# A hybrid decoder step on one core: another chunk order in round one, another place for the spatial products, top-ks given out together, other PSUM for the key transpositions, and weight splits off GpSimd

## The chip, the cores and the metric

The kernel runs on one core of a Trainium2 chip. The metric is the device time of one execution in microseconds (us). The engines are PE (matrix products; PEld is its weight load), DVE (vector), ACT (scalar functions), POOL (GpSimd) and SP (which here only issues DMAs). Each engine works through its own list of instructions in order, and waits on semaphores where it needs another's result.

## The reference

One layer of a decoder step for 2048 prompt rows and 64 sample rows (8 sequences of 8), model width 1024, in float32:

```
z = rmsnorm(x) @ w_in                     # q, k, v, index queries qi, index key ki, index weights wi, ga, u, vm, gm
score = sum_h wi_h * relu(qi_h . ki)      # 8 index heads of 64
idx = top_k(causal score, 256)            # per query row
o = softmax attention of 8 heads over the chosen keys (4 key heads, QK norm, partial rotary)
s = W_s (lower triangular 128 x 128, per group) @ layernorm(gelu(vm)) + b_s
gm_out = gelu(u) * s * silu(gm)
r = x + [o * silu(ga), gm_out] @ w_out
y = r + sigmoid(rmsnorm(r) @ w_ple_gate) * (p @ w_ple_proj)
```

The outputs are y for both sets of rows, the new k, v and index keys, and the layernormed vm of the sample rows.

## The kernel before, in words

**Phase A, projection.** The 16 prompt blocks of 128 rows and the sample block (SB) are done in three rounds (`ROUNDS`). In each round the columns of w_in are taken in 14 chunks (`CH`): x1, x2 (index key and queries), vm0, vm1, k, v, u0, u1, gm0, gm1, q0, q1, ga0, ga1. A chunk has 256 columns, x1 has 328 from two places of w_in. Every float32 product is made of halves rounded to the PE's fp32r and their remainders: `proj` issues 24 matmuls for one block and chunk (16 at L319 and L320, 8 at L322), and 16 for SB (L312, L313). In round one `load_w` fetches each chunk as 8 raw tiles (L282, five buffers), and splits each into the high half (L286 on ACT for every second tile of the first chunk, L288 on POOL otherwise) and the low half (L289 on DVE); later rounds reload the halves from DRAM. `split_h` transposes the rows of x (L250). `post` finishes a chunk: for v one ACT copy and a store (L409); for q0, q1 and k a square, a sum (L389), two small POOL steps (L390, L391), two products (L396, L397) and the rotary part (L133 to L136).

`spatial(g)` makes one group's spatial products (L338, L343) between the projections: four groups in the chunk v, four in u0.

**Index work.** From the end of x2 `pump` gives out, after each block and by a credit, index products of the due blocks (L688, L689 on PE, relu L691 on ACT, accumulation L693 on DVE) and top-ks (`topk`: seven counts, L829 on ACT with small DVE steps between them, then MAX8 at L865 and a mask, L875, whose store goes to `s_mask`).

**End of phase A.** The products of the gm columns with w_out follow (`gm_split` L567, `gm_product` L579 to L583, eviction L585, store L588). At the ninth, `pump(1e9)` gives out all that is left of the index work, and `prep_early` begins: per key block loads (L991, L992, two buffers each), a doubling copy on ACT (L1015), four transpositions on PE (L1021), evictions into Kst on ACT (L1023) and DVE (L1024), and two POOL steps for the values (L1026, L1027, tile Vst). The transposes take their PSUM from the pool `tp`, two buffers, which `gm_split` uses too. Kst and Vst lie where the index work's tiles lay. A flag (L897, L902) sums up the top-ks' counts.

**Phase B** is the attention over query blocks; **phase C** the product with w_out, the norm, and the gate, whose ten weight tiles `raw_split` (L1421 on ACT, L1423 and L1424 on POOL or DVE) splits between the blocks, and where POOL adds the residual (L1437).

The program's order is only the scheduler's input: the framework simulates the program's times and writes each engine's list from that.

Of the kernel before, what the change touches and what calls it, by code (L numbers as in the profile page):

```python
# [9 lines left out]
F32 = mybir.dt.float32  # L10
# [44 lines left out]
Q_POOL = [0, 0, 1]  # L55
ROUNDS = [[0, 1, 2, 3, 4, SB], [5, 6, 7, 8, 9, 10], [11, 12, 13, 14, 15]]
DUE = ROUNDS[:2] + [ROUNDS[2][::-1]]
CH = [
# [53 lines left out]
class Builder:  # L112
# [85 lines left out]
    def phase_a(self, eb):  # L198
        tc, nc, I, O = self.tc, self.nc, self.I, self.O
        with ExitStack() as es:  # L200
# [68 lines left out]
            def load_w(ci, r):  # L269
# [8 lines left out]
                for k in range(8):  # L278
# [5 lines left out]
                    g = self.gk[:, k:k + 1]  # L284
                    if ci == 0 and k % 2:
                        nc.scalar.activation(wh[:, k], raw, AF.Copy, scale=g)  # L286
                    else:
                        nc.gpsimd.tensor_scalar(wh[:, k], raw, g, 1.0, op0=OP.mult, op1=OP.mult)  # L288
# [163 lines left out]
            def pump(budget):  # L452
                credit[0] = min(credit[0], 0.0) + budget
                while credit[0] > 0 and (blocks_due or primed or dots or tops):
# [10 lines left out]
                    if l:  # L465
                        try:
                            v = next(l[0])
                            steps[0] += l is dots
                            if isinstance(v, tuple):
                                tops.append(self.topk(*v))  # L470
                                v = 0
                            credit[0] -= v
                            if l is tops and not (dots or primed or blocks_due):
# [3 lines left out]

            seq = [(r, c) for r in range(len(ROUNDS)) for c in range(len(CH))]
            load_x(ROUNDS[0][0])
            W0 = load_w(0, 0)  # L480
            split_h(ROUNDS[0][0])
# [10 lines left out]
            for si, (r, c) in enumerate(seq):  # L492
                blocks = ROUNDS[r]
                name = CH[c][0]
# [31 lines left out]
                for j, b in enumerate(blocks):  # L526
# [9 lines left out]
                    post(name, b, z)  # L536
                    g = {"v": j + 4 - len(blocks), "u0": 4 + j if j < 4 else -1}.get(name, -1)
                    if g >= 0:
# [11 lines left out]
                cur = nxt  # L550
                if c == 1:
                    blocks_due += [b for b in DUE[r] if b >= 2]
                    tot = sum((b + 1) * 18 + 8 if b < SB else 110 for b in blocks if 2 <= b)
                    self.idx_rate = tot / (RATE[r] * len(blocks))
# [37 lines left out]
            for n in range(0, 17, 2):  # L592
# [5 lines left out]
                for j in range(2):  # L598
                    for b in order[n:n + 2]:
# [9 lines left out]
                        if u == DRAIN:  # L609
                            pump(1e9)  # L610
                            ei.close()
                            early = self.prep_early(eb, lambda: self.tp.tile([128, 4, 128], F32, name="tp"))
                        if u == FLAG_AT:
# [777 lines left out]
    def phase_c(self):  # L1391
# [3 lines left out]
        with ExitStack() as es:  # L1395
# [145 lines left out]
            for n in range(LEAD + 1):  # L1541
# [3 lines left out]
                for q in range(n * per, min(n * per + per, len(gates))):  # L1545
                    raw_split(*gates[q], nc.gpsimd if q % 3 == 2 else nc.scalar, nc.gpsimd if q % 3 == 1 else V)
                    if q + 3 < len(gates):
                        raw_load(*gates[q + 3])
# [38 lines left out]
```

## Time and profile before

| | us |
|---|---|
| median of 3 runs | 1889.77 (1889.49 to 1900.7) |
| the profiled execution's own time | 1893.5 |
| its span | 1891.7 |
| PE busy in the span | 1833.5 (97%) |
| mean granted PE clock | 0.988 of 2.4 GHz |
| chain that ended last | PE 83%, DVE 5%, DMA 5%, POOL 2%, issue 2%, ACT 2% |

The profile shows one execution. PE's busy time is counted from modelled ends, so a busy PE can still run at the lower of its two clock levels; the column for the clock tells that. Times in the rows count from the first instruction of the span.

### The profile page before, as it was taken

What the parts mean: (1) busy time and instruction counts of PE and PEld (TensorE: products, weight loads), DVE (VectorE), ACT (ScalarE), POOL (GpSimd) and SP (SyncE); (2) the same over time, 40 slices, a digit from 0 to 9 for tenths busy, and PEclk for the clock granted to TensorE, in tenths of its full rate; (3) what the DMA queues carried; (4) which work ended last, traced back from release to release, by engine and by line L of the source; (5) the groups of instructions that cost most, each with busy time, mean ns of one, the idle gap of its engine ahead of it and who ended that gap; (6) DMA issues with size and microseconds to landing.
All of it is one profiled execution on the core that took longest, in us unless ns stands there. A gap on an engine that the chain in (4) does not pass through costs nothing.

```text
span 1891.7 us, 33962 instructions
## 1 busy us (share of the span) xinstructions
PE 1833.5 (97%) x11974; PEld 1601.0 (85%) x11974; DVE 1242.1 (66%) x3631; ACT 1018.2 (54%) x1909; POOL 623.5 (33%) x950
## 2 busy tenths in 40 slices
PE   7989998999999999999988899999999999999998
PEld 7989988999999999999877678778777777888887
DVE  5597665378878547788752789888999764233321
ACT  4244335256565636766654888868788653122121
POOL 5482562342012324013303442233221364222221
PEclk9989999999999999999999899999999999999999
DMA  8855756645344554554553442233220373223211
GB/s 253 247 163 179 223 189 203 215 131 161 119 162 146 194 174 145 163 170 134 176 188 128 134 112 76 64 108 94 61 78 12 100 258 122 74 95 104 94 37 45
DMA packets 243806, 261.53 MB, mean 138 GB/s; under 512 B 83176, under 2 KB 209840, under 8 KB 243248
## 3 DMA queue, kind: packets, MB, share of 16 engines
q1 hardware_dynamic: 237744, 240.45, 40.5%
q0 software_dynamic: 5888, 18.88, 3.4%
q8 instruction: 95, 1.56, 0.3%
q14 instruction: 79, 0.65, 0.1%
HBM read 171.90 MB, written 87.37 MB: 137 GB/s over the span
## 4 chain that ended last, share of the span: by engine, by line
PE 83%; DVE 5%; DMA 5%; POOL 2%; issue 2%; ACT 2%; SPq 0%; DVEq 0%; POOLq 0%; ACTq 0%
PE z L319 10%; PE z L320 10%; PE z L322 10%; PE b_o L1155 7%; PE b_tp L1138 6%; PE c_mm L1471 5%; PE c_mm L1470 5%; PE c_mm L1474 5%; PE b_s L1103 3%; PE dots L688 3%; PE dots L689 3%; PE b_s L1104 3%; PE z L579 1%; PE z L580 1%; PE z L583 1%
## 5 line engine op out<-in xcount | busy, mean ns | idle before, releaser
L319 PE MATMUL z<-whi,hhi 128*128 128x256 f32 (+1 forms) x1792 | 463.0, 292 | 10.5 <-ACT vt L414 5.0
L320 PE MATMUL z<-wlo,hhi 128*128 128x256 f32 (+1 forms) x1792 | 454.1, 287 | 0.2 <-DVE wlo L289 0.2
L319 PEld LDWEIGHTS z<-whi,hhi 128*128 128x128 f32 x1792 | 341.9, 191 | 21.2 <-issue 8.5
L320 PEld LDWEIGHTS z<-wlo,hhi 128*128 128x128 f32 x1792 | 341.8, 191 | 6.1 <-DVE wlo L289 1.5
L322 PE MATMUL z<-whi,hlo 128*128 128x256 f32 (+1 forms) x1792 | 262.6, 286 | 0.0
L322 PEld LDWEIGHTS z<-whi,hlo 128*128 128x128 f32 x1792 | 237.7, 190 | 2.0
L693 DVE SCALAR_TENSOR_TENSOR big<-dots,sgn,big 128x1024 f32<-128x1024 f32 (+7 forms) x176 | 179.2, 1018 | 52.3 <-ACT dots L691 50.6
L125 DVE TENSOR_TENSOR b_pt<-b_tp,b_pt 128x512 fp32r<-128x512 f32 (+1 forms) x288 | 183.4, 655 | 12.1 <-ACT b_pt L124 11.0
L691 ACT ACTIVATE dots<-dots 128x1024 f32<-128x1024 f32 (+7 forms) x176 | 140.3, 801 | 87.7 <-PE dots L689 82.9
L1155 PE MATMUL b_o<-b_pt,Vst 128*128 128x512 f32 x544 | 184.1, 424 | 1.2 <-DVE b_pt L125 0.8
L124 ACT ACTIVATE b_pt<-b_tp 128x512 fp32r<-128x512 f32 (+1 forms) x288 | 155.5, 578 | 48.2 <-PE b_tp L1138 45.4
L1138 PE MATMUL b_tp<-mats,b_sm 128*128 128x128 f32 x1088 | 172.0, 275 | 2.3 <-DVE b_pt L125 1.8
L1112 ACT ACTIVATE b_sm<-b_sm,b_st 128x128 f32<-128x128 f32 (+15 forms) x128 | 154.7, 1210 | 16.2 <-DVE b_st L1105 15.4
L829 ACT ACTIVATE bfw<-big,tk 128x384 bf16<-128x384 f32 (+14 forms) x105 | 136.4, 1300 | 45.7 <-DVE tk L849 27.9
L1138 PEld LDWEIGHTS b_tp<-mats,b_sm 128*128 128x128 f32 x1088 | 131.5, 141 | 34.1 <-ACT b_sm L1112 4.8
L1103 PE MATMUL b_s<-Kst,b_qh 128*128 128x512 f32 (+3 forms) x320 | 139.5, 439 | 4.1 <-DVE b_st L1105 2.2
L1105 DVE CUSTOM_DVE_ANT_0 b_sm<-b_s,b_mask,b_st 128x512 f32<-128x512 f32 (+3 forms) x192 | 123.9, 646 | 22.6 <-PE b_s L1104 17.8
L1104 PE MATMUL b_s<-Kst,b_ql 128*128 128x512 f32 (+3 forms) x320 | 117.6, 370 | 0.0
L688 PE MATMUL dots<-ki_stack,qih 128*128 128x512 f32 (+3 forms) x304 | 113.0, 373 | 3.1 <-DVE mk L833 3.1
L689 PE MATMUL dots<-ki_stack,qil 128*128 128x512 f32 (+3 forms) x304 | 110.2, 371 | 0.0
L1471 PE MATMUL c_mm<-c_l_w_ple_gate,c_mh 128*128 128x512 f32 x272 | 106.7, 392 | 3.2 <-DVE c_l_w_ple_gate L1424 2.1
L1470 PE MATMUL c_mm<-c_h_w_ple_gate,c_mh 128*128 128x512 f32 x272 | 109.0, 401 | 0.0
(351 smaller groups left out, 3747.0 us busy)
## 6 DMA issues: line engine op xcount, KB each, us to landing
whi<-s_wh SPq DMA_DIRECT2D x52, 512.0 KB
wlo<-s_wl SPq DMA_DIRECT2D x52, 512.0 KB
raw<-w_in SPq DMA_DIRECT2D x112, 128.0 KB
s_wh<-whi SPq DMA_DIRECT2D x13, 1024.0 KB
s_wl<-wlo SPq DMA_DIRECT2D x13, 1024.0 KB
b_qr<-s_q SPq DMA_DIRECT2D x32, 256.0 KB
s_r<-hlo SPq DMA_DIRECT2D x32, 256.0 KB
c_r<-s_r SPq DMA_DIRECT2D x16, 512.0 KB
```

What stands on the lines that cost most here:

```text
L125: nc.vector.tensor_tensor(lo, src, hi.bitcast(F32), OP.subtract)
L319: nc.tensor.matmul(z, lhsT=hh[:, k], rhs=wh[:, k, :n], start=(k == 0), stop=False)
L320: nc.tensor.matmul(z, lhsT=hh[:, k], rhs=wl[:, k, :n], start=False, stop=False)
L322: nc.tensor.matmul(z, lhsT=hl[:, k], rhs=wh[:, k, :n], start=False, stop=(k == 7))
L688: nc.tensor.matmul(ps[:, s0:s0 + sn], lhsT=qh[h // 4][:, h % 4], rhs=rhs, start=True, stop=False)
L693: nc.vector.scalar_tensor_tensor(a, r, self.sgn[:, b, h:h + 1], a, op0=OP.mult, op1=OP.add)
L1103: nc.tensor.matmul(ps, lhsT=qh[:, h], rhs=rhs, start=True, stop=False)
L1104: nc.tensor.matmul(ps, lhsT=ql[:, h], rhs=rhs, start=False, stop=True)
L1138: nc.tensor.transpose(ps[:, k, r], sm2[r][:, (k0 + k) * 128:(k0 + k) * 128 + 128], ident)
L1155: nc.tensor.matmul(o.rearrange("p a b -> p (a b)"), lhsT=Vst[:, kb, g].rearrange("p a d -> p (a d)"), rhs=pt[:, k].rearrange("p a b -> p ( ...
L1470: nc.tensor.matmul(z, lhsT=hi[:, k], rhs=wts[k][0][:, ns], start=(k == 0), stop=False)
L1471: nc.tensor.matmul(z, lhsT=hi[:, k], rhs=wts[k][1][:, ns], start=False, stop=(b == SB and k == nk - 1))
```

## The change

It has six edits. In round one the chunks come in the order `FIRST`: v, x1, x2, vm0, vm1, k, q0, u0, u1, gm0, gm1, q1, ga0, ga1; rounds two and three keep theirs. In round one four spatial groups are called in q0, not in v. The index work still begins behind x2, which is now the third chunk; the constants that were made in the second and third chunk (index constants; `gmlp_weights`, `page_rows` with L190 and L191) are now made in x1 and x2. A step of `pump` is not charged to the credit once no index products are left. The key transpositions take their PSUM from the index products' pool (`dots`, two buffers). All ten weight tiles of phase C are split by ACT (high half) and DVE (low half).

```diff
--- before.py
+++ after.py
@@ -54,6 +54,7 @@
 WLO_DVE = [6, 5, 0]
 Q_POOL = [0, 0, 1]
 ROUNDS = [[0, 1, 2, 3, 4, SB], [5, 6, 7, 8, 9, 10], [11, 12, 13, 14, 15]]
+FIRST = [5, 0, 1, 2, 3, 4, 10, 6, 7, 8, 9, 11, 12, 13]
 DUE = ROUNDS[:2] + [ROUNDS[2][::-1]]
 CH = [
     ("x1", [(1536, 72), (1024, 256)]),
@@ -282,7 +283,7 @@
                         nc.sync.dma_start(raw[:, o:o + cn], I["w_in"][0, k * 128:(k + 1) * 128, c0:c0 + cn])
                         o += cn
                     g = self.gk[:, k:k + 1]
-                    if ci == 0 and k % 2:
+                    if ci == FIRST[0] and k % 2:
                         nc.scalar.activation(wh[:, k], raw, AF.Copy, scale=g)
                     else:
                         nc.gpsimd.tensor_scalar(wh[:, k], raw, g, 1.0, op0=OP.mult, op1=OP.mult)
@@ -469,15 +470,16 @@
                             if isinstance(v, tuple):
                                 tops.append(self.topk(*v))
                                 v = 0
-                            credit[0] -= v
+                            if dots or primed or blocks_due:
+                                credit[0] -= v
                             if l is tops and not (dots or primed or blocks_due):
                                 tops.append(tops.pop(0))
                         except StopIteration:
                             l.pop(0)
 
-            seq = [(r, c) for r in range(len(ROUNDS)) for c in range(len(CH))]
+            seq = [(r, c) for r in range(len(ROUNDS)) for c in (range(len(CH)) if r else FIRST)]
             load_x(ROUNDS[0][0])
-            W0 = load_w(0, 0)
+            W0 = load_w(FIRST[0], 0)
             split_h(ROUNDS[0][0])
             load_x(ROUNDS[0][1])
             ropet = ac.tile([128, 17, 32], F32, name="ropet")
@@ -534,7 +536,7 @@
                         f()
                     later.clear()
                     post(name, b, z)
-                    g = {"v": j + 4 - len(blocks), "u0": 4 + j if j < 4 else -1}.get(name, -1)
+                    g = {"v" if r else "q0": j + 4 - len(blocks), "u0": 4 + j if j < 4 else -1}.get(name, -1)
                     if g >= 0:
                         spatial(blocks, g)
                     if name == "ga1":
@@ -548,7 +550,7 @@
                         keep_w(c, cur)
                     pump(self.idx_rate)
                 cur = nxt
-                if c == 1:
+                if name == "x2":
                     blocks_due += [b for b in DUE[r] if b >= 2]
                     tot = sum((b + 1) * 18 + 8 if b < SB else 110 for b in blocks if 2 <= b)
                     self.idx_rate = tot / (RATE[r] * len(blocks))
@@ -609,7 +611,8 @@
                         if u == DRAIN:
                             pump(1e9)
                             ei.close()
-                            early = self.prep_early(eb, lambda: self.tp.tile([128, 4, 128], F32, name="tp"))
+                            early = self.prep_early(eb, lambda: self.dp.tile([128, 1024], F32, name="dots")[:, :512]
+                                                    .rearrange("p (a b) -> p a b", a=4))
                         if u == FLAG_AT:
                             self.flag(self.tp.tile([128, 4, 128], F32, name="tp")[:, 0])
                 for b in order[n + 2:n + 4]:
@@ -1543,7 +1546,7 @@
                 stage1b(blocks[n])
                 stage1a(blocks[n + 1])
                 for q in range(n * per, min(n * per + per, len(gates))):
-                    raw_split(*gates[q], nc.gpsimd if q % 3 == 2 else nc.scalar, nc.gpsimd if q % 3 == 1 else V)
+                    raw_split(*gates[q], nc.scalar, V)
                     if q + 3 < len(gates):
                         raw_load(*gates[q + 3])
             for n in range(2):
```

Lines of the changed kernel are one to three higher than those of before: L1021 is L1024 there, L567 is L569, L992 is L995.

On SP, the start of the program: x is the rows of a block (`big` holds two of them), raw a piece of the chunk's weights. Before:

```order
L232 DMA x_253<-x_prompt 128x1024
L282 DMA raw_257<-w_in 128x72
L282 DMA raw_257<-w_in 128x256
...
L282 DMA raw_292<-w_in 128x72
L282 DMA raw_292<-w_in 128x256
L232 DMA x_318<-x_prompt 128x1024
L484 DMA ropet_320<-c_rope 128x544
L232 DMA big_322<-x_prompt 128x1024 x2
L232 DMA big_325<-x_prompt 128x1024
L232 DMA big_325<-x_sample 64x1024
```

and now:

```order
L233 DMA x_253<-x_prompt 128x1024
L283 DMA raw_257<-w_in 128x256
...
L283 DMA raw_273<-w_in 128x256
L233 DMA x_310<-x_prompt 128x1024
L486 DMA ropet_312<-c_rope 128x544
L233 DMA big_314<-x_prompt 128x1024
L283 DMA raw_277<-w_in 128x256
L283 DMA raw_281<-w_in 128x256
L283 DMA raw_285<-w_in 128x256
L233 DMA big_314<-x_prompt 128x1024
L233 DMA big_317<-x_prompt 128x1024
L233 DMA big_317<-x_sample 64x1024
```

The first chunk is 8 transfers where it was 16, and the second block's rows are asked for ahead of the last three of them.

On PE, the end of phase A: `tp` and `dots` with one source b_kd are key transpositions (L1021, now L1024), `tp` from hlo the transposes of gm (L567, now L569), each z the first matmul of one of the w_out products of 12. Before:

```order
L1021 MATMUL tp_13027<-mats_60,b_kd_12993 128x128 x4
L579 MATMUL z_12870<-whi_12555,hhi_12815 128x512
...
L579 MATMUL z_12939<-whi_12399,hhi_12923 128x512
...
L579 MATMUL z_13040<-whi_12555,hhi_12931 128x512
...
L1021 MATMUL tp_13059<-mats_60,b_kd_13025 128x128 x4
L567 MATMUL tp_13073<-mats_60,hlo_13023 128x128 x4
L567 MATMUL tp_13081<-mats_60,hlo_13055 128x128 x4
L579 MATMUL z_13088<-whi_12399,hhi_13072 128x512
...
L1021 MATMUL tp_13105<-mats_60,b_kd_13057 128x128 x4
L579 MATMUL z_13118<-whi_12399,hhi_13080 128x512
...
L1021 MATMUL tp_13135<-mats_60,b_kd_13103 128x128 x4
```

and now:

```order
L1024 MATMUL dots_13027<-mats_60,b_kd_12993 128x128 x4
L581 MATMUL z_12838<-whi_12399,hhi_12815 128x512
...
L569 MATMUL tp_13073<-mats_60,hlo_13023 128x128 x4
...
L581 MATMUL z_12978<-whi_12399,hhi_12931 128x512
...
L569 MATMUL tp_13213<-mats_60,hlo_13163 128x128 x4
...
L581 MATMUL z_13180<-whi_12555,hhi_13080 128x512
...
L900 MATMUL tp_13398<-f_sm_13410 1x1
L1024 MATMUL dots_13059<-mats_60,b_kd_13025 128x128 x4
L1024 MATMUL dots_13105<-mats_60,b_kd_13057 128x128 x4
L581 MATMUL z_13228<-whi_12399,hhi_13212 128x512
...
L581 MATMUL z_13258<-whi_12399,hhi_13220 128x512
...
L1024 MATMUL dots_13135<-mats_60,b_kd_13103 128x128 x4
```

Between the second and the third key transposition stood five products, and stand eleven with six gm transposes; the third now follows the flag's product (`tp_13398`), and from there the keys come in pairs.

On SP, the same stretch: b_kr are key loads, b_vr value loads, s_r the products' stores. Before:

```order
L876 DMA s_mask_174<-bfw_12225 128x1536
L992 DMA b_vr_13005<-v_prompt 128x256
L992 DMA b_vr_13037<-v_prompt 128x256
L991 DMA b_kr_13144<-k_prompt 128x256
L992 DMA b_vr_13069<-v_prompt 128x256
...
L992 DMA b_vr_13209<-v_prompt 128x256
L588 DMA s_r10_167<-hlo_13023 128x512
L991 DMA b_kr_13176<-k_prompt 128x256
L992 DMA b_vr_13255<-v_prompt 128x256
L992 DMA b_vr_13285<-v_prompt 128x256
```

and now:

```order
L879 DMA s_mask_174<-bfw_12107 128x1536
L590 DMA s_r11_168<-hlo_13055 128x512
L995 DMA b_vr_13005<-v_prompt 128x256
...
L995 DMA b_vr_13115<-v_prompt 128x256
...
L994 DMA b_kr_13144<-k_prompt 128x256
...
L994 DMA b_kr_13176<-k_prompt 128x256
...
L995 DMA b_vr_13285<-v_prompt 128x256
L994 DMA b_kr_13208<-k_prompt 128x256
L994 DMA b_kr_13254<-k_prompt 128x256
...
L995 DMA b_vr_13395<-v_prompt 128x256
L994 DMA b_kr_13284<-k_prompt 128x256
```

The key loads still stand among the value loads of later blocks, in pairs now.

## Rows read from the trace of the kernel before

**Rows 1.** The page, part 1: busy us, share of the span, instructions.

```profile
PE 1833.5 (97%) x11974; PEld 1601.0 (85%) x11974; DVE 1242.1 (66%) x3631; ACT 1018.2 (54%) x1909; POOL 623.5 (33%) x950
```

**Rows 2.** PE's waits: line and tile, for what; us in total, times, longest.

```profile
PE tp L1021 <- DVE Kst L1024: 7.3, 2, 6.2
...
PE z L319 <- ACT vt L414: 5.0, 2, 2.5
...
PE tp L567 <- DVE Kst L1024: 3.4, 3, 1.8
...
PE dots L688 <- DVE mk L833: 3.1, 1, 3.1
...
PE z L319 <- DVE vt L316: 2.7, 1, 2.7
...
PE c_mm L1471 <- DVE c_l_w_ple_gate L1424: 2.1, 1, 2.1
...
PE c_mm L1471 <- POOL c_l_w_ple_gate L1424: 1.2, 1, 1.2
```

**Rows 3.** Timeline, SP's DMA issues at the start: start us, duration us, work.

```profile
2.28 8.27 SPq L282 DMA_DIRECT2D raw<-w_in  x16
...
10.60 0.43 SPq L232 DMA_DIRECT2D x<-x_prompt  x1
```

**Rows 4.** Timeline, PE at the start: the first block's first matmul, the next block's transposes.

```profile
7.72 0.61 PE L319 MATMUL z<-whi,hhi 128*128 128x328 f32 x1
...
17.30 1.06 PE L250 MATMUL tp<-mats,x 128*128 128x128 f32 x4
```

**Rows 5.** Windows: length, busy PE, PEld, DVE, ACT, POOL, then clock, DMA share, GB/s.

```profile
40.50:62.00 21.50, 16.65 (x107) 15.47 (x108) 13.21 (x43) 2.62 (x8) 12.46 (x31) 0.78 0.81 246
...
140.00:160.00 20.00, 20.00 (x158) 18.97 (x157) 15.00 (x72) 7.95 (x21) 7.78 (x12) 1.00 0.69 213
...
160.00:200.00 40.00, 40.00 (x311) 36.99 (x310) 30.15 (x132) 19.53 (x44) 9.30 (x17) 1.00 0.53 169
...
262.00:285.00 23.00, 23.00 (x160) 18.89 (x158) 15.29 (x49) 7.68 (x20) 12.71 (x19) 1.00 0.53 164
...
980.50:1045.10 64.60, 51.16 (x248) 41.21 (x247) 22.23 (x49) 27.47 (x51) 18.02 (x32) 0.92 0.37 121
```

**Rows 6.** Timeline, DVE: the addition for the sample rows of the first chunk.

```profile
43.55 0.49 DVE L316 TENSOR_TENSOR vt<-z,vt 64x328 f32<-64x328 f32 x1
```

**Rows 7.** Windows of the instructions on tile qn in 262 to 285: DVE, ACT, POOL.

```profile
262.00:285.00 23.00, 8.11 (x31) 2.84 (x6) 0.00 (x0) 1.00 0.53 164
```

**Rows 8.** The same window, instructions on tile qst: DVE, POOL.

```profile
262.00:285.00 23.00, 4.46 (x11) 7.47 (x11) 1.00 0.53 164
```

**Rows 9.** Timeline, PE: two key transpositions and the product between them.

```profile
993.51 0.60 PE L1021 MATMUL tp<-mats,b_kd 128*128 128x128 f32 x4
...
993.87 0.48 PE L579 MATMUL z<-whi,hhi 128*128 128x512 f32 x1
...
996.69 0.60 PE L1021 MATMUL tp<-mats,b_kd 128*128 128x128 f32 x4
```

**Rows 10.** Timeline, DVE: the first key evictions.

```profile
986.03 1.30 DVE L1024 TENSOR_TENSOR Kst<-tp,Kst 64x512 fp32r<-64x512 f32 x2
```

**Rows 11.** Tile b_vr: ns least, median, most; first and last start.

```profile
L1026 POOL TENSOR_SCALAR Vst<-b_vr x16: 397/404/406, 988.2 to 1015.4; 128x256 fp32r<-128x256 f32 x16
```

**Rows 12.** Timeline, SP: the issue of one key load.

```profile
1000.42 0.42 SPq L991 DMA_DIRECT2D b_kr<-k_prompt  x1
```

**Rows 13.** Timeline, ACT: the copy that waited for this load.

```profile
1003.55 0.62 ACT L1015 COPY b_kd<-b_kr 128x512 f32<-128x512 f32 x1 [2.39 <-DMA b_kr<-k_prompt]
```

**Rows 14.** Timeline, DVE: two low halves of phase C's weights.

```profile
1541.60 1.22 DVE L1424 TENSOR_TENSOR c_l_w_ple_gate<-c_raw,c_h_w_ple_gate 128x1024 fp32r<-128x1024 f32 x1
...
1559.69 3.38 DVE L1424 TENSOR_TENSOR c_l_w_ple_gate<-c_raw,c_h_w_ple_gate 128x1024 fp32r<-128x1024 f32 x1 [0.94 <-POOL c_h_w_ple_gate L1423]
```

**Rows 15.** Timeline, POOL: the addition beside the second of them.

```profile
1559.62 2.36 POOL L1437 TENSOR_TENSOR c_x<-c_x,c_r 128x1024 f32<-128x1024 f32 x1
```


## The prediction

> **What bounds the kernel now.** I read the page first: PE is busy for 1833.5 of 1891.7 us [rows 1], so only its 58 us of idle time, and the time in which it is busy at the lower of its two clock levels (1.2 instead of 2.4 GHz), can be won; an engine that is relieved elsewhere wins nothing. Then PE's list of waits, which says where the idle time lies [rows 2]. It is spread: the largest entries are key transpositions and gm transposes that wait for the key evictions (7.3 + 3.4 us, up to 6.2 at once), projections behind the s_ga stores (5.0), an index product in round one (3.1), a projection behind the sample rows of x1 (2.7), and phase C's gate products (2.1 + 1.2). Then the windows of the places that the change touches, where the reader is to compare PE's busy time with the length and look at the clock [rows 5], and the timelines around each of them.
>
> The sum is made against the profiled execution, 1893.5 us (span 1891.7), which is 3.7 us above the median of the three runs; I take the difference over to the median. A measurement of this kernel can tell about 1% from no change, that is 18.9 us.
>
> **Start, v as the first chunk.** SP spends from 2.28 to 10.55 us on the sixteen raw transfers of x1, and asks for the second block's rows only at 10.60 [rows 3]. The first block's 24 matmuls therefore last from 7.72 to 17.30, 9.58 us [rows 4]. In v there are 8 transfers, the second block's rows go ahead of the last three, and a matmul has 256 columns where it had 328: 9.58 x 256/328 = 7.5, a gain of 2.1 from the columns alone. But x1 is not gone, only second, and its columns are paid later; what is won is waiting time, not columns. I take +2, with bounds 0 (the weights come no faster) and 4.
>
> **The sample rows of x1.** In 40.5 to 62, PE is busy for 16.65 of 21.50 us, at a mean clock of 0.78 [rows 5]: 4.85 us idle, and about 0.22 x 16.65 = 3.7 us lost to the clock, 8.5 in all. The step that ended last is the addition for SB at 43.55 on DVE [rows 6], which in DVE's list stood behind the page rows (L190, L191) and low halves of the next weights; PE was stopped for 2.7 us of that [rows 2]. In the changed order the first chunk ends in ACT copies, x1 is second, and the page rows are made a chunk later, in x2. The stop for SB should go, but the same small work is still to be done in the first 80 us, so something is late elsewhere. I take +3, bounds -1 and 7.
>
> **Spatial products from v to q0.** Their number is unchanged, and so is their place relative to k, the chunk ahead. The 3.1 us stop of the index products behind a count's DVE step [rows 2] belongs to that place too, and I cost it at nothing. What is new is that q0 stands where v stood. v costs DVE nothing there; q0 costs, per block, six of the 31 instructions on qn, 8.11/31 x 6 = 1.57 us, and one sum, of the 4.46 us on qst, about 0.41 [rows 7, 8]: 1.98, for six blocks 11.9 us. POOL gets 7.47/11 x 2 = 1.36 per block, 8.1 in all [rows 8]. In the 20 us of v's chunk DVE is busy for 15.0, in the 40 us behind it for 30.2 [rows 5]. 15.0 + 11.9 = 26.9 us do not fit in 20; 57.0 fit into the 60, barely. The 6.9 us that are too much must slip into the next chunk. PE is kept waiting as far as two z buffers don't cover it, and each stop also costs clock. I take -4; the bounds are -12 (6.9 and as much again of low clock) and +2 (all covered, and a gap at k's end closed by the shift). Where q0 was, PE had no idle time to give back (23.00 of 23.00 busy at clock 1.00 [rows 5]): nothing returns there.
>
> By the Trainium skill (SBUF — State Buffer, section "SBUF: two separate sides") a DVE instruction with two SBUF inputs and a GpSimd instruction that reads SBUF exclude each other for their whole length. By that, q0 could cost DVE up to POOL's 1.36 us more per block, 8 us in six, and this term would be -12. The rows of q0's old place speak against so much: there the same DVE work ran beside the same POOL work at 8.11/31 = 0.26 us an instruction, and PE never stopped [rows 5, 7, 8].
>
> **Unchanged places.** The stops behind the s_ga stores and the first small blocks of phase B have the same work and the same queues: nothing.
>
> **Credit.** The last top-ks are given out together. The last one is a chain of counts, each waiting for the one before, and its start is set by the last index product, which doesn't move. Nothing, bounds -2 and 2.
>
> **End of phase A.** This is the main term. In 980.5 to 1045.1, PE is busy for 51.2 of 64.6 us, at a clock of 0.92 [rows 5]. The work in it is 12 products of 2.82 us (993.87 to 996.69), 14 key transpositions and 7 gm transposes of 0.36 each (993.51 to 993.87) [rows 9], and two sample products that I put at 1.9: 33.8 + 7.6 + 3.8 = 45.2 us. So 19.4 us are lost. The cause is the PSUM: the first two key transpositions hold both `tp` buffers until the first key evictions on DVE at 986.03 [rows 10], which come only when the last top-k is through and its memory is free. Until then neither a third key nor a gm transpose can start, and the products run out.
>
> With the keys in `dots`, the gm transposes have `tp` for themselves. The order of the changed kernel puts eleven products and six transposes between the second and third key, 11 x 2.82 + 6 x 0.36 = 33 us from about 961, so that PE comes to the third key near 994, some 8 us after the first evictions. From there 14 key transpositions are left, 8 products and two for the samples: 14 x 0.36 + 8 x 2.82 + 3.8 + 0.4 = 32 us. Everything at full speed would end near 1026, 19 us earlier.
>
> What is late next would be the key loads, since they stand on SP among value loads, whose buffers come free only by POOL's steps for the values: sixteen starts from 988.2 to 1015.4, 1.8 us apart [rows 11]. A key takes 3.1 us from its issue to its copy (1000.42 to 1003.55) [rows 12, 13]. SP's new order shows the closest case: the loads of the ninth and tenth key (b_kr_13208 and the next) stand behind the eleventh value's (b_vr_13285), which with two buffers waits for the ninth value step, 988.2 + 9 x 1.8 = 1004.4; they can be used near 1008. PE gets to them near 994 + 6 x 0.36 + 5 x 2.82 = 1010. That holds, with little in hand. I take +14 of the 19.4: 5 us for waits that an order doesn't show. Bounds 6 (the keys hold up each pair by 2 us) and 19.
>
> **Phase C.** The two waits of the gate products are 2.1 and 1.2 us [rows 2]. POOL no longer splits, so it starts its additions earlier, and the raw buffers come free earlier. DVE has three more low halves of 1.22 us, ACT three more high halves; both have room there. I take +3, bounds 1 and 4. The wait of 2.1 us ended with a low half on DVE that took 3.38 where another took 1.22 [rows 14], while POOL added the residual for 2.36 beside it [rows 15]; the lower bound is for a low half that still meets an addition and is 2.2 late. The same page and section of the Trainium skill speaks against this edit, since POOL keeps its additions and all low halves now go to the engine that they exclude. The trace agrees here (3.38 against 1.22 + 2.36); by the rule of the Trainium skill alone this term would be +1.
>
> **Sum.** 2 + 3 - 4 + 0 + 14 + 3 = 18 us. The profiled execution would take 1893.5 - 18 = 1875.5, and the median 1889.8 - 18 = 1872 us, 0.95% less.
>
> **The rivals.**
> - *DVE becomes the bound in q0* (slower than before). If the products of q0 find no free z, PE runs its 20 us at half clock, 20 us lost. For it: DVE's load of 26.9 in 20 us, and the clock that falls at each stop, as in 40.5 to 62 [rows 5]. Against it: the scheduler may spread the work, and q0's old place ran with no idle time. With 2 for the early terms together, 13 at the end of A and 1 in phase C: 2 - 20 + 13 + 1 = -4, about 1894. It decides once DVE's work per block, index work included, exceeds what PE takes for one, 20/6 = 3.3 us. The rule of the Trainium skill quoted above (SBUF — State Buffer) points the same way. Chance 0.10.
> - *The stop moves to the key loads.* The value steps wait for the last mask's store, so the loads can begin no earlier than before; if each pair then waits 2 us, the end of A brings 6, and the sum is 10: 1880. Chance 0.16.
> - *All of it works.* 19 at the end of A, 3 + 5 early, 0 in q0, 3 in C: 30, or 1860. For it: the order puts 8 us between the evictions and the third key. Chance 0.20.
> - *The change doesn't do what it says.* The engines' orders come from simulated times; if these err as they did before, stops of the same size come at other places, and only C's 3 us remain: 1887. Chance 0.10.
> - The forecast, with its own range of 1865 to 1879: chance 0.44.
>
> **The numbers.** 1872 us. The range for 8 in 10 is 1858 to 1888: it leaves out the slow rival and a part of the best one. Faster by over 1% means below 1870.9: the whole of the third rival and half of the forecast's case, with a little of the rest, 0.44. Slower by over 1% needs more than 1908.7: the first rival with every other term at its low end, 0.03. The rest, 0.53, is within 1%.
>
> **What would show it.** In the profile after: the wait of the key transpositions for Kst is gone or below 2 us, and the stretch from the last top-k's MAX8 to phase B's first score is near 50 us, not 64.6. In q0's chunk of round one PE has idle time and a lower clock, with DVE over 9 tenths. The first block takes about 7.5 us. The gate products wait for under 1 us. The forecast is wrong if the gm products in turn wait for their own evictions or loads, or if the q0 stop exceeds 12 us.

## The result, and the profile after

The changed kernel takes 1877.5 us in the median of 8 runs (1875.3 to 1881.5), the kernel before in the same series 1892.2; the ratio is 0.9919 with a 95% interval from 0.9904 to 0.9935, so 0.8% less, 14.7 us, where 18 were forecast. The profiled execution takes 1878.1 us, its span 1876.1.

Part 1 of its page, against [rows 1]:

```profile
PE 1826.7 (97%) x11974; PEld 1595.9 (85%) x11974; DVE 1243.8 (66%) x3634; ACT 1018.5 (54%) x1912; POOL 607.3 (32%) x944
```

PE's work is the same 11974 matmuls; its span is 15.6 us shorter. PE's list of waits, against [rows 2] (line numbers are one to three higher):

```profile
PE z L320 <- DVE qn L380: 3.9, 2, 2.9
...
PE dots L691 <- DVE mk L836: 2.5, 1, 2.5
...
PE z L320 <- ACT vt L410: 2.3, 1, 2.3
...
PE c_mm L1473 <- ACT c_ph L125: 2.2, 1, 2.2
...
PE c_mm L1474 <- DVE c_l_w_ple_gate L1427: 1.2, 2, 0.8
```

From the last top-k's MAX8 (979.88) to phase B's first score (1025.94) it takes 46.1 us, where it took 64.5. No wait for Kst is left, where there were 7.3 + 3.4 us, and the s_ga wait (vt L414, 5.0 us) is gone from the head of the list; in their place stand small stops of round one (L380, L410) and a new one in phase C, for c_ph. The windows that answer to [rows 5], with 300 to 320 added:

```profile
40.50:62.00 21.50, 18.23 (x117) 17.33 (x117) 10.93 (x45) 5.22 (x22) 9.90 (x24) 1.00 0.85 283
...
160.00:200.00 40.00, 39.56 (x300) 36.53 (x299) 33.29 (x149) 20.76 (x50) 20.75 (x29) 1.00 0.55 174
...
300.00:320.00 20.00, 19.46 (x161) 18.64 (x160) 4.42 (x15) 8.60 (x21) 2.15 (x6) 1.00 0.60 208
...
980.50:1026.00 45.50, 44.99 (x231) 36.62 (x229) 17.56 (x43) 24.14 (x46) 18.16 (x32) 1.00 0.52 171
```

and that stretch in the kernel before, where two stops of 2.5 us lay:

```profile
300.00:320.00 20.00, 15.04 (x122) 14.63 (x121) 8.73 (x50) 11.78 (x24) 1.02 (x3) 0.97 0.78 265
```

To see where time came from and went, I set against each stretch what its matmuls would take at full speed (for each shape of matmul the spacing that three in ten of them undercut in the trace of before) and call the rest lost. This is an estimate. Its gains add up to 15.5 of the 15.6 us, but with the matmuls sorted by their tiles as well, single rows move by up to 1 us. The recorded expectations below count by a rougher sorting: they have 4.8 and 10 where the table has 5.2 and 10.1 for the start of phase C.

| stretch (times of before) | lost before | lost after | gain | forecast |
|---|---|---|---|---|
| 0 to 20 | 13.8 | 10.8 | 3.0 | 2 |
| 20 to 100 | 10.2 | 14.8 | -4.6 | 3 |
| 100 to 160 | 10.4 | 8.8 | 1.6 | 0 |
| 160 to 280 | 8.6 | 8.5 | 0.1 | -4 |
| 280 to 340 | 8.2 | 4.2 | 4.0 | 0 |
| 340 to 920 | 9.7 | 10.5 | -0.8 | 0 |
| 920 to phase B (1045; after 1026) | 20.3 | 4.6 | 15.7 | 14 |
| phase B | 70.3 | 69.3 | 1.0 | 0 |
| phase C, first 42 us | 5.2 | 10.1 | -4.9 | 3 |
| the rest | 11.2 | 10.8 | 0.4 | 0 |

The main term came nearly as forecast. That the sum did too is in part luck: x1 and phase C came 7.6 and 7.9 us short of their terms, and q0 (4.1), the end of round one (4.0) and smaller rows made up for most of that.

### The profile page after: what moved, and what is told of

Same layout as the page of the kernel before. It is cut to its first block, busy times and chain, and to the rows that moved or that the text cites. A ratio compares the mean times of both kernels' runs of the same rounds, so it can differ in the third digit from the quotient of the medians.

```text
span 1876.1 us, 33944 instructions
## 1 busy us (share of the span) xinstructions
PE 1826.7 (97%) x11974; PEld 1595.9 (85%) x11974; DVE 1243.8 (66%) x3634; ACT 1018.5 (54%) x1912; POOL 607.3 (32%) x944
## 5 line engine op out<-in xcount | busy, mean ns | idle before, releaser
L126 DVE TENSOR_TENSOR b_pt<-b_tp,b_pt 128x512 fp32r<-128x512 f32 (+1 forms) x288 | 183.1, 654 | 12.0 <-ACT b_pt L125 11.2
L1158 PEld LDWEIGHTS b_o<-b_pt,Vst 128*128 128x128 f32 x544 | 89.3, 189 | 22.6 <-DVE b_pt L126 7.3
```

What stands on the lines that cost most here:

```text
L126: nc.vector.tensor_tensor(lo, src, hi.bitcast(F32), OP.subtract)
L1158: nc.tensor.matmul(o.rearrange("p a b -> p (a b)"), lhsT=Vst[:, kb, g].rearrange("p a d -> p (a d)"), rhs=pt[:, k].rearrange("p a b -> p ( ...
```

## The experiments

**The PSUM edit alone** (kernel before, one edit):

```diff
-early = self.prep_early(eb, lambda: self.tp.tile([128, 4, 128], F32, name="tp"))
+early = self.prep_early(eb, lambda: self.dp.tile([128, 1024], F32, name="dots")[:, :512].rearrange(...))
```

> The kernel before with one edit, the key transpositions in the index products' PSUM. Theory: this edit alone gives what the end of phase A gained, 17 us: about 1875 against 1892, the stretch from MAX8 of the last top-k to phase B's first score near 46 us instead of 64.6. Rival: the gain needs the credit edit too (all top-ks given out at once, so that the last one ends earlier); then the gain here is below 10 us, and key transpositions or evictions still wait for the last top-k.

Measured: 1873.7 us (1871.9 to 1878.7), ratio 0.9897 [0.986, 0.9933]. The 49 us ahead of phase B's first score, with the same columns:

```profile
982.00:1031.00 49.00, 48.53 (x247) 39.57 (x245) 21.05 (x45) 25.51 (x48) 18.15 (x32) 1.00 0.52 164
```

PE is busy for 48.5 of 49 us at full clock, no key transposition waits, and from MAX8 (984.98) to the first score (1031.04) it takes 46.1 us, as the theory has it. This edit alone gives as much as the whole change, within what the runs can tell.

**The credit edit undone** in the changed kernel:

```diff
-if dots or primed or blocks_due:
-    credit[0] -= v
+credit[0] -= v
```

> The changed kernel without the credit edit: the last top-ks are given out step by step. Theory: the last top-k is a chain of counts whose start its last index product sets, so nothing changes beyond 2 us, and its MAX8 ends at 981 to 983 as before. Rival: the credit edit is part of what the end of phase A gained; then this is 4 or more us slower.

Measured: 1878.3 us (1875.4 to 1881.0), ratio 0.9922 [0.9897, 0.9947], the time of the changed kernel. The last MAX8 starts at 981.1, in the changed kernel at 979.9. The edit is worth nothing that can be measured; the end of phase A is the PSUM's.

**Round one's edits alone** (v first, products in q0, index work behind x2 as third chunk):

```diff
-seq = [(r, c) for r in range(len(ROUNDS)) for c in range(len(CH))]
+seq = [(r, c) for r in range(len(ROUNDS)) for c in (range(len(CH)) if r else FIRST)]
-g = {"v": j + 4 - len(blocks), ...
+g = {"v" if r else "q0": j + 4 - len(blocks), ...
```

> The kernel before with the edits of round one alone: v first, x1 second, spatial products in q0, index work behind x2 as third chunk. Theory: the early stops move but are not saved (0 us by 300), and the stops behind the s_ga stores at 300 to 320 go, because the index work now reaches to the round's last chunks: 3 to 6 us faster than before, about 1888, with 5 us of PE's waits for ACT vt L414 gone. Rival of the prediction: the early part gains by itself and the s_ga stops, which come from the DMA traffic, are chance; then the waits for vt stay at 5 us.

Measured: 1891.1 us, ratio 0.9999 [0.9981, 1.0017]. The stops behind the s_ga stores are gone (0.6 us left), and PE runs through:

```profile
300.00:320.00 20.00, 20.00 (x167) 19.37 (x168) 5.11 (x16) 9.11 (x21) 2.60 (x7) 1.00 0.64 220
```

By 340 us this execution has lost 6.0 us less than the kernel before, by 920 only 2.3 less: it loses 13.5 us in rounds two and three, where before loses 9.7. Over all profiles but the two with another `RATE`, eight executions with round one's new order had lost 45.0 to 51.8 us by 340 (mean 48.2) and 54.4 to 64.2 by 920 (mean 59.0); four with the old order 48.1 to 51.4 (mean 50.3) and 59.8 to 63.1 (mean 61.2). So about 2 us stay, less than the scatter between executions, and the times of ten runs show nothing of them.

**Does the end of the index work remove the s_ga stops?** In the kernel before with `RATE[0]` 12 for 11 (index work lasts a chunk longer), and in the changed kernel with 10 (a chunk shorter):

```diff
-RATE = [11, 11, 11]
+RATE = [12, 11, 11]   # in the kernel before; [10, 11, 11] in the changed one
```

> The kernel before with one number changed: the index work of round one is given out in twelfths of a chunk's blocks instead of elevenths, so that it ends with the last chunk, not one chunk earlier. Theory: index products then stand between the blocks of ga0 and ga1, the s_ga stores have time to land, and the two stops of 2.5 us at 306 and 318 go or shrink under 1 us each: 3 to 6 us faster. Rival: the stops come from the DMA traffic of the weights that are written and loaded there, and stay: 0 to 1 us.

> The changed kernel with the index work of round one given out in tenths of a chunk's blocks, so that it ends one chunk before the round, as it did in the kernel before. Theory: PE then has nothing beside the projections in ga0 and ga1, and the stops behind the s_ga stores come back, 3 to 5 us in 290 to 330. Rival: those stops depend on the traffic, which is the same; they stay away, and the time is that of the changed kernel within 2 us.

Measured: 1896.0 us, ratio 1.0019 [1.0003, 1.0034], with twelfths; 1878.8 us (1874.3 to 1880.8) with tenths. In their times both theories miss: no gain in the one (0.2% more), no loss in the other. The traces say more. With twelfths 280 to 340 loses 4.2 us where before loses 8.2, but 160 to 280 loses 13.8 where before loses 8.6, for a stop has come at 278, in the q chunks:

```profile
278.32 0.58 PE L319 MATMUL z<-whi,hhi 128*128 128x256 f32 x1 [5.04 <-ACT qn L393]
```

(the ACT copy before it waited for the store to s_q). With tenths in the changed kernel 280 to 340 loses 7.2 us where the changed kernel loses 4.2, though only 1.3 us of it is a wait for vt; two waits of 1.0 us are the next round's row transposes, behind DVE. So in these four executions the round's end loses 4 us where the index work lasts to it and 7 to 8 where it doesn't; over all, it loses 3.5 to 5.2 in the eight with round one's new order, and 5.6 to 8.2 in the four with the old one. With twelfths those 4 us are not won but moved, to another store.

**Phase C's edit undone** in the changed kernel, twice:

```diff
-raw_split(*gates[q], nc.scalar, V)
+raw_split(*gates[q], nc.gpsimd if q % 3 == 2 else nc.scalar, nc.gpsimd if q % 3 == 1 else V)
```

> The changed kernel with phase C's splits as they were before (two of ten high halves and three low halves more on POOL). Theory: the edit of phase C costs time, because POOL keeps its residual additions and a low half on DVE that meets one takes 3.4 us instead of 1.2; DVE is then the bound of the gate stretch. Then this kernel is 3 to 5 us faster than the changed one (about 1873 where that has 1877.5), and its gate products wait as they did before (2.1 + 1.2 us) without the low clock of 1545 to 1555. Rival: the loss in phase C is the clock's alone, chance from run to run, or belongs to the start of phase C; then it stays within 1 us of the changed kernel and shows a low clock in the same places.

> The changed kernel with phase C's splits as they were before, timed again with more rounds, as the version to keep. Theory: the collisions of phase C are what it is spared, so it is again 3 to 6 us faster than the changed kernel: 0.988 to 0.990 of the kernel before. Rival: the 5.7 us of its first timing were the chip's; then the ratio is that of the changed kernel, 0.991 to 0.993.

Measured: first 1871.8 us (1871.4 to 1875.2), ratio 0.9889 [0.9854, 0.9925]; again 1878.1 us (1874.6 to 1879.1), 0.9921 [0.9909, 0.9932]. (The edit gives POOL three of ten high halves back, not two, as the first expectation has it.) The second run takes back what the first seemed to show: the times alone don't tell this kernel from the changed one. Phase C's first 42 us do: the two executions lose 7.2 and 5.2 there, all six with the old splits 5.2 to 7.2, where the changed kernel loses 10.1.

Not all of that belongs to the splits. In six of the fourteen executions, the changed kernel's among them, the clock of the first 6 us is only 0.72 to 0.74, and 1.5 to 1.7 us are lost there; the others lose 0.1. Three of the six have the old splits, and in the changed kernel the first low half starts only at 1524.12, so this loss isn't the edit's; no run shows where it comes from. Before, and the changed kernel:

```profile
1533.00:1539.00 6.00, 6.00 (x28) 4.93 (x29) 1.22 (x2) 2.50 (x3) 3.64 (x3) 1.00 1.02 386
```

```profile
1512.80:1518.80 6.00, 6.00 (x21) 4.73 (x22) 1.26 (x2) 0.60 (x1) 2.63 (x2) 0.72 1.00 369
```

In the 36 us behind them the six with the old splits lose 3.5 to 5.7, the changed kernel 8.4. The second execution came to its last MAX8 at 983.7, the changed kernel's at 979.9, so its time was lost ahead of phase C.

**Phase C's edit alone** (kernel before):

> The kernel before with phase C's edit alone. Theory: low halves on DVE meet POOL's additions as in the changed kernel, and the stretch of 42 us from phase C's first product loses 8 to 10 us where it lost 4.8: 3 to 5 us slower than before. Rival: the edit is worth the 3 us that were predicted, and the changed kernel's loss came with the order of its lists, which another order need not have (the kernel with tenths lost only 2.6 us there with the same edit); then this is up to 3 us faster than before.

Measured: 1889.9 us, ratio 0.9991 [0.9979, 1.0003]. The theory fell, the rival stands: the stretch loses only 1.8 us, 3.4 less than before, though the time doesn't show it beyond its interval. No low half was held up, all took 1.2 us (least, median and most in ns):

```profile
L1424 DVE TENSOR_TENSOR c_l_w_ple_gate<-c_raw,c_h_w_ple_gate x8: 1211/1217/1224, 1539.3 to 1560.1; 128x1024 fp32r<-128x1024 f32 x8
```

Not that they met no addition. Three of POOL's additions met one and took 3.37, 2.71 and 3.29 us, where the median of all seventeen is 2.39: there the low half had started first, and the addition waited. The last of them, on DVE and POOL:

```profile
1556.46 1.21 DVE L1424 TENSOR_TENSOR c_l_w_ple_gate<-c_raw,c_h_w_ple_gate 128x1024 fp32r<-128x1024 f32 x1
```

```profile
1556.65 3.29 POOL L1437 TENSOR_TENSOR c_x<-c_x,c_r 128x1024 f32<-128x1024 f32 x1 [4.60 <-DMA c_r<-s_r]
```

Once an addition held up another DVE instruction (c_rn at 1549.72, 3.42 us). PE waited for none of these.

**What the collisions are.** In the changed kernel: the residual additions left out for five blocks; the same additions on DVE; every third low half back on POOL; and, with the additions on DVE, the kernel before with the PSUM edit and phase C's.

```diff
-nc.gpsimd.tensor_tensor(x, x, r, OP.add)
+if b not in blocks[1:6]:                      # residuals left out
+    nc.gpsimd.tensor_tensor(x, x, r, OP.add)
+(V if b in blocks[1:6] else nc.gpsimd).tensor_tensor(x, x, r, OP.add)   # or: on DVE
```

> The changed kernel, with POOL's residual addition left out for the five blocks that follow the first in phase C (their rows of y miss the product of the gm columns). Theory: DVE's low halves are slow only where they meet such an addition; without it all ten take 1.2 us, DVE is no longer busy from end to end in 1540 to 1555, and the 10 us that the stretch of 42 us from phase C's first product loses against full speed fall to 5 or less: 4 to 6 us faster than the changed kernel. Rival: the loss comes from the three more high halves on ACT, which hold up the transposed p (PE's wait of 2.2 us for c_ph); then the stretch stays as it is.

> The changed kernel with the residual additions of the five blocks after phase C's first moved from POOL to DVE, so that nothing on POOL meets the low halves. Theory: each addition costs DVE 1.2 us where a collision cost it 2.2, every low half takes 1.2, and the stretch of 42 us from phase C's first product loses 5 us or less against full speed instead of 10: about 1872, as with the splits of before, perhaps better. Rival: DVE's load alone is the bound there (ten low halves and five additions, 18 us more than the norms); then the stretch loses 8 us or more and the time stays at 1876 to 1880.

> The kernel before with the key transpositions in the index products' PSUM, phase C's splits on ACT and DVE, and the five residual additions on DVE; round one and the credit as before. Theory: round one's edits are worth nothing within 3 us, so this is within 3 us of the changed kernel with the additions on DVE. Rival: round one's 6 us by 340 stay won; then this is 5 or more us slower than that.

> The changed kernel with half of phase C's edit: all ten high halves on ACT, but every third low half on POOL, as before. Theory: the low halves on DVE are what costs, so this is near the kernel with phase C as before (1872), or 1 to 2 us better, since POOL loses its three high halves of 2 us. Rival: ACT's high halves cost; then it stays at 1876 to 1878.

Measured, in this order: 1873.0 us (two runs), ratio 0.9897 [0.9865, 0.9929], the stretch loses 2.7 us; 1873.1 us (1867.2 to 1881.2), ratio 0.9914 [0.9888, 0.9939], 2.9 us; 1873.9 us (1872.7 to 1874.6), ratio 0.9902 [0.9885, 0.9918], 4.5 us (1.5 of them in the first 6); 1878.1 us (1877.5 to 1882.5), 0.9932 [0.9907, 0.9956], 9.0 us. The intervals of the first three overlap that of the changed kernel, so it is the stretch that speaks. With no addition on POOL beside them the low halves take 1.2 us each and the stretch runs nearly full, though in two of these kernels DVE does the additions too; so neither DVE's load nor ACT's high halves are the cause. The third kernel, without round one's edits and the credit's, is within 1 us of the second, as its theory has it. The last kernel's forecast missed, and its time is the one that the rival gave, but ACT's ten high halves stand in the other three too. With a third of the low halves on POOL the collisions stay, on both engines: PE stops for 2.3 us behind a low half on POOL and for 1.8 behind two on DVE.

The same 42 us from phase C's first product, in seven executions (columns as in [rows 5]; the first count is that of matmuls). Before, and the changed kernel:

```profile
1533.00:1575.00 42.00, 38.44 (x180) 30.70 (x181) 28.82 (x25) 16.07 (x24) 32.96 (x20) 1.00 0.70 253
```

```profile
1512.80:1554.80 42.00, 38.11 (x154) 29.33 (x155) 32.45 (x26) 17.96 (x25) 16.62 (x13) 0.88 0.67 246
```

The changed kernel without the credit edit, and with tenths:

```profile
1514.20:1556.20 42.00, 37.90 (x153) 29.44 (x154) 32.44 (x26) 17.96 (x25) 16.27 (x13) 0.88 0.67 242
```

```profile
1516.50:1558.50 42.00, 41.00 (x192) 32.91 (x193) 31.04 (x29) 21.39 (x29) 18.30 (x14) 1.00 0.73 255
```

Phase C's edit alone, additions on DVE, and the old splits again:

```profile
1531.80:1573.80 42.00, 41.54 (x195) 33.77 (x196) 29.84 (x30) 21.47 (x29) 18.26 (x14) 1.00 0.73 255
```

```profile
1508.90:1550.90 42.00, 40.48 (x189) 32.59 (x190) 31.48 (x33) 21.58 (x29) 7.80 (x10) 1.00 0.73 253
```

```profile
1518.40:1560.40 42.00, 39.92 (x180) 31.90 (x181) 24.37 (x25) 17.71 (x26) 31.00 (x19) 0.96 0.69 240
```

The reader is to see three things. In the same time PE does 180 matmuls before, 154 in the changed kernel, 195 with the edit alone (7 of the 26 that the changed kernel lacks are lost in the first 6 us). Of these seven the clock is lowest, 0.88, where PE falls furthest behind. And the kernel without the credit edit does what the changed one does (153), while the one with tenths, which has the same edit too, does 192. All instructions of phase C stand in the same order on all five engines in the changed kernel and in the one without the credit edit; in the one with tenths and in the edit-alone kernel the order is another, and the same one in both. So how much the same edit costs goes with the order of the lists, in two executions of either order. The order doesn't settle it alone: of the two executions of the old splits, which are one program, the first holds up a low half that the second doesn't. Of these two low halves in a row one takes 3.4 us in the first execution, and PE stops for 2.65 us behind it:

```profile
1540.42 4.51 DVE L1427 TENSOR_TENSOR c_l_w_ple_gate<-c_raw,c_h_w_ple_gate 128x1024 fp32r<-128x1024 f32 x2
```

```profile
1546.82 2.35 DVE L1427 TENSOR_TENSOR c_l_w_ple_gate<-c_raw,c_h_w_ple_gate 128x1024 fp32r<-128x1024 f32 x2
```

## Why the prediction was right, and where it was not

**End of phase A.** The step was right, and a little small: 14 were taken and 15.7 came. From the last MAX8 to phase B's first score 19.2 us were lost before, and 2.3 are now. The rows for it are the third key behind the gm transposes, as the order had it, and the evictions well ahead of it, against [rows 9, 10]:

```profile
988.78 0.60 PE L569 MATMUL tp<-mats,hlo 128*128 128x128 f32 x4
...
992.17 1.09 PE L1024 MATMUL dots<-mats,b_kd 128*128 128x128 f32 x8
```

```profile
979.88 1.75 DVE L868 MAX8 v<-big 128x8 f32<-128x1536 f32 x1
...
987.61 1.30 DVE L1027 TENSOR_TENSOR Kst<-dots,Kst 64x512 fp32r<-64x512 f32 x2
```

The first evictions start 1.6 us later than before (987.61), but PE comes to the third key only at 992.17, and the window of 45.5 us above answers to the 45.2 us of work that were worked out. Most of the 5 us that I held back for waits that an order doesn't show were not needed: the key loads kept pace. The edit alone in the kernel before shows that this step carries the change.

**Start and sample rows of x1.** The start gained 3.0 us for 2: SP's first five transfers take 2.33 us and the second block's rows follow at 4.65, where they came at 10.60 [rows 3].

```profile
2.28 2.33 SPq L283 DMA_DIRECT2D raw<-w_in  x5
...
4.65 0.43 SPq L233 DMA_DIRECT2D x<-x_prompt  x1
```

The first block didn't shrink to 7.5 us, as the sum over the columns had it. Its first matmul starts at 9.15 and its last eight not before 17.15, so it takes some 9 us; what is won is that the second block's first matmuls already stand among them:

```profile
9.15 0.55 PE L320 MATMUL z<-whi,hhi 128*128 128x256 f32 x1 [1.16 <-ACT hhi L125]
...
17.15 1.12 PE L323 MATMUL z<-whi,hlo 128*128 128x256 f32 x8
```

The 3 us for x1 failed. The step was that the stop belonged to the page rows ahead of the addition; that one went, and in 40.5 to 62 PE is busy for 18.23 of 21.50 us at clock 1.00, where it was 16.65 at 0.78. But others came at 35 (L410 behind v's store), 57 and 63 (L380), and 4.6 us more are lost by 100. The one at 57 belongs to the page rows again, a chunk later: DVE waits 2.67 us for the page table before them, and qn, which PE needs, stands behind them.

```profile
35.03 0.64 PE L320 MATMUL z<-whi,hhi 128*128 128x328 f32 x1 [2.35 <-ACT vt L410]
...
57.58 0.39 PE L313 MATMUL z<-whi,hhi 128*128 128x328 f32 x1 [1.73 <-DVE qn L380]
```

```profile
55.14 0.51 DVE L192 TENSOR_SCALAR prow<-pt,off 64x32 int32<-64x32 int32 x2 [2.67 <-DMA pt<-page_table]
...
57.01 0.42 DVE L380 TENSOR_TENSOR qn<-z,absw 128x256 f32<-128x256 f32 x1
```

I had written that the same small work is still to be done and something would be late elsewhere, and yet took 3 us.

**q0.** -4 was too much: 160 to 280 loses 8.5 us where it lost 8.6. DVE is busy for 33.29 of 40 us in 160 to 200, where 37.1 were reckoned (30.2, and the 6.9 that slip over), and PE for 39.56 at clock 1.00. So the sign that was named for this term, idle time and a lower clock with DVE over 9 tenths, did not come. Why DVE's load stayed below the reckoning is open. Presumably the two z buffers took up the rest; no run tested it. Nor does each stop cost clock, as the term assumed: the kernel before has stops of 2.1 and 1.2 us in phase C, in 42 us at clock 1.00.

By the Trainium skill (SBUF — State Buffer, section "SBUF: two separate sides") POOL's steps could have cost DVE 8 us more here, by the prediction's estimate. The trace shows no such loss: within one POOL step of 1.02 us (L392, from 171.00) two of DVE's products start at 171.50 and take 0.74 us together.

**Unchanged places.** "The same work and the same queues: nothing" failed: the round's end gained 4.0 us, where the index work now lasts to its last chunks. I had read that the index work starts a chunk later and did not follow what that fills at the other end. Over all executions about 2 us of it stay, less than they scatter.

**Phase C.** The sign was wrong in the changed kernel: +3 was taken, -4.9 came, of which 1.6 are the low clock of the first 6 us. That the edit can gain is right, as its stretch in the edit-alone kernel shows (+3.4 in one execution). What failed is the lower bound: I let one low half meet one addition, at 2.2 us. The price was right and the count wrong: four of ten do, on DVE and POOL:

```profile
1524.12 5.69 DVE L1427 TENSOR_TENSOR c_l_w_ple_gate<-c_raw,c_h_w_ple_gate 128x1024 fp32r<-128x1024 f32 x3 [2.16 <-ACT c_h_w_ple_gate L1424]
...
1536.39 3.42 DVE L1427 TENSOR_TENSOR c_l_w_ple_gate<-c_raw,c_h_w_ple_gate 128x1024 fp32r<-128x1024 f32 x1
...
1545.53 3.37 DVE L1427 TENSOR_TENSOR c_l_w_ple_gate<-c_raw,c_h_w_ple_gate 128x1024 fp32r<-128x1024 f32 x1
...
1552.02 3.18 DVE L1427 TENSOR_TENSOR c_l_w_ple_proj<-c_raw,c_h_w_ple_proj 128x1024 fp32r<-128x1024 f32 x1
```

```profile
1524.05 2.40 POOL L1440 TENSOR_TENSOR c_x<-c_x,c_r 128x1024 f32<-128x1024 f32 x1
...
1535.78 2.95 POOL L1440 TENSOR_TENSOR c_x<-c_x,c_r 128x1024 f32<-128x1024 f32 x1 [0.63 <-DMA c_r<-s_r]
...
1544.71 3.11 POOL L1440 TENSOR_TENSOR c_x<-c_x,c_r 128x1024 f32<-128x1024 f32 x1 [1.58 <-DMA c_r<-s_r]
...
1551.74 2.38 POOL L1440 TENSOR_TENSOR c_x<-c_x,c_r 128x1024 f32<-128x1024 f32 x1 [3.92 <-DMA c_r<-s_r]
```

Three low halves in a row take 5.69 where 3.6 would do, and three more 3.42, 3.37 and 3.18. Each of the four starts less than 1 us behind an addition, and the last three end 1.08 us behind the end of theirs, which is nearly what they take alone. In the edit-alone kernel it is the other way round: there the addition shown ends 2.27 us behind the end of its low half. In these rows the two don't share: the one that starts second waits for the first to end.

DVE has no gap from 1539.7 to 1555, so the raw buffers come free late (a load is issued at 1542.11, as the low half of 1540.87 ends); ACT waits for this load, the transposed p (c_ph) stands behind that on ACT, PE stops for 2.2 us, and then runs eight matmuls in 3.61 us that took 2.0 before:

```profile
1546.01 1.06 ACT L1424 ACTIVATE c_h_w_ple_proj<-c_raw 128x1024 fp32r<-128x1024 f32 x1 [1.56 <-DMA c_raw<-w_ple_proj]
...
1546.97 0.36 ACT L125 ACTIVATE c_ph<-c_tp 128x256 fp32r<-128x256 f32 x1
```

```profile
1547.39 0.79 PE L1473 MATMUL c_mm<-c_h_w_ple_proj,c_ph 128*128 128x512 f32 x1 [2.19 <-ACT c_ph L125]
...
1549.55 3.61 PE L1477 MATMUL c_mm<-c_h_w_ple_gate,c_ml 128*128 128x512 f32 x8
```

The rule of the Trainium skill that was weighed there (SBUF — State Buffer, section "SBUF: two separate sides": of a DVE instruction with two SBUF inputs and a GpSimd instruction that reads SBUF, the one that starts first holds the other off for its whole length) agrees with these rows, 3.42 against 1.21 alone, and priced the term nearer than my own sum. What it cannot tell is how often they meet and which starts first; for that I had to look at the order of the lists, which I did only for phase A.

**Not settled.** The two executions of the old splits, one program, come to the last MAX8 at 979.3 and 983.7, and the eight with round one's order at 975.5 to 985.7; no run here separates the cause. The low clock at phase C's start in six of the executions is as open. So which of the versions with the PSUM edit is best stays open: the PSUM edit alone, the one with the additions on DVE on top of it (1873.9) and the old splits (1871.8 and 1878.1) have intervals that overlap that of the changed kernel.

## What to carry to other kernels

When a tile can't be evicted until other work has freed its memory, don't let it hold PSUM that the work in between needs: one edit that took another pool was worth as much as the whole change, within what the runs can tell. When work is moved off an engine, look in the written order for what the receiving engine's two-input instructions will stand beside on GpSimd, since a low half that started just behind an addition took 2.2 us longer (one alone takes 1.2); where it started first, only the addition waited, and PE lost nothing. And where execution times scatter by more than the effect, measure the stage: matmuls done in a fixed window told 154 from 180 where the times told nothing. Look inside the window too: 7 of those 26 were lost at its start, where the edit had no part.

## What was not expected of the hardware

A DVE subtraction of 128 x 1024 floats from SBUF takes 1.21 to 1.23 us alone and 3.2 to 3.4 when it starts just behind a GpSimd addition of the same size. The addition takes 2.4 alone and up to 3.4 when it starts just behind the subtraction. Beside GpSimd's steps of 4 elements a row, DVE's products of 256 elements in q0 kept their 0.4 us.

PE's granted clock in phase C's first 42 us was 0.88 in the changed kernel (154 matmuls), but 1.00 before (180), though the two longest stops are alike in both: 2.2 and 0.8 us, and 2.1 and 1.2. A part of the changed kernel's lower clock lies in the first 6 us, at 0.72 with PE busy throughout.
